# Float32 streaming-encoder trunk on one core: first products copied from PSUM to PSUM, one sum of weight quarters by an adding DMA, and the pools' first products moved

## The chip, the cores and the metric

The kernel runs on one core of a Trainium2 chip. The metric is device time of one execution in microseconds (us). Three executions of the kernel before took 709.14 to 709.78 us, median 709.22. TensorE (PE in the profile) multiplies 128x128 weight tiles with moving columns into PSUM, eight banks of 128x512 float32 each. VectorE (DVE), ScalarE (ACT) and GpSimd (POOL) work on elements; SyncE (SP) issues most DMAs.

## The reference

One layer over x of 512 tokens and 1024 channels, all in float32:

```
h = rmsnorm(x, norm_g)
a_u, a_v, a_z, b_p, b_z, c_h, c_b, c_c, c_z, gate_logits = split(h @ w_in)   # 9 x 1024 and 3 x 1024 columns
ya = spatial_gating(gelu(a_u), gelu(a_v), ...) * silu(a_z)
yb = multiscale_pool(b_p, pool_w, ...) * silu(b_z)      # trailing means over 2, 4, 8, 16 tokens, minus p, times pool_w
yc = c_b * causal_depthwise_conv(c_c * c_h, ...) * silu(c_z)
gates = sigmoid(gate_logits)                            # one of 1024 columns per branch
merged = gates_a * (ya @ w_branch_a) + gates_b * (yb @ w_branch_b) + gates_c * (yc @ w_branch_c)
out = rmsnorm(x + merged @ w_out, final_g)
```

## The kernel before, in words

Each float32 factor is split into a high part (hi, written by ScalarE as a cast, L59) and a low part (lo, the rest, written by VectorE, L60). A product is then three matmuls: hi by hi, hi by lo and lo by hi.

The wide product h @ w_in (except a_v) is made in 22 groups by `group` (L426 to L491). A group takes 2 x 128 output columns from each half of a 1024-column block, over all 1024 inputs, in a form with seven products instead of eight. Its weights are four quarters, a11, a12, a21 and a22, 128x1024 elements and 512 KB each, loaded by SyncE into the pool `wraw` (seven buffers, L62 to L65). The activations stand ready as seven combinations (b11, b21, t1 to t4, b22), each hi and lo. VectorE makes the combinations of weights: s1 = a21 + a22, a21' = a11 - a21, a11' = s1 - a11, a12' = a12 - a11' (L453 and L454). ScalarE and VectorE split each quarter or combination into `whi` and `wlo`, four buffers each. Each of the seven products is 24 matmuls of 256 columns (L437 to L443).

In order: b11 into bank px; ScalarE copies px to SBUF (c1, L447); b21 into its own bank py; VectorE adds c1 to py into the first quarter of the output (`plus`, L451); t2 is added on px, and ScalarE copies that (c2); t1 into pz; t3 added on px, copied (c3); VectorE adds c3 to pz; b22 added on pz, then c2 is added; t4 added on px, which ScalarE writes out. `use` (L483 to L490) is what a group does with its output: an activation by ScalarE, or, for cc, a product by VectorE.

`run` (L493) interleaves the groups: the b11 of a group comes before the late products b22 and t4 of the group ahead of it. Between some groups stand "other" steps: the mixing products of the branches. The order of groups is au0, az0, mix, au1, az1, mix, gates a0 with mixes, bp0, gates a1 with mixes (numbers 0 to 6, `mix` not counted), then bz0, bp1, pools' small products 0, bz1, pools' small products 1, gates b0 and b1 with mixes (7 to 11), then the eight groups of branch c (12 to 19) and its gates (20, 21). At the end come the product with w_out and the final norm. The instructions of each engine are put in order by the scheduler of the framework, which works from the dependences and its own estimates; only what goes through `pin` (the start) keeps the written order.

The pools (L654 to L675) are VectorE work on the output of bp; a pool's small product `pool_mm` (L685 to L710) is twelve matmuls, followed by two VectorE instructions and one of ScalarE for each tile. `keep_busy` (L157 to L161) is a run of matmuls of ones at the start.

Of the kernel before, what the change touches and what calls it, by code (L numbers as in the profile page):

```python
# [8 lines left out]
F32 = mybir.dt.float32  # L9
F32R = mybir.dt.float32r  # L10
AF = mybir.ActivationFunctionType
ALU = mybir.AluOpType
PSUM = bass.MemoryType.PSUM

P = 128
D = 1024
S = 512
KT = D // P
NB = S // P
HALF = 512  # L20
GC = 256
# [9 lines left out]
def mixers_kernel(ctx, tc, x, norm_g, w_in, sgu_ln_g, sgu_ln_b, sgu_w, sgu_b, pool_w, pool_b, pool_scale,  # L31
                  conv_w, conv_b, w_branch_a, w_branch_b, w_branch_c, w_out, final_g, out):
    nc = tc.nc
# [11 lines left out]
    wsum = ctx.enter_context(tc.tile_pool(name="wsum", bufs=2))  # L45
    whi = ctx.enter_context(tc.tile_pool(name="whi", bufs=4))
    wlo = ctx.enter_context(tc.tile_pool(name="wlo", bufs=4))
    outs = ctx.enter_context(tc.tile_pool(name="outs", bufs=3))
    part = ctx.enter_context(tc.tile_pool(name="part", bufs=3))
    tmp = ctx.enter_context(tc.tile_pool(name="tmp", bufs=4))  # L50
    small = ctx.enter_context(tc.tile_pool(name="small", bufs=4))
    psum = ctx.enter_context(tc.tile_pool(name="psum", bufs=8, space=PSUM))

    def bank():
        return psum.tile([P, 512], F32, tag="ps", name="ps")

    def split(hi, lo, src, keep=lambda ins: ins):

# [3 lines left out]
    def load_raw(src, shape):  # L62
        raw = wraw.tile([P, *shape], F32, tag="wraw", name="wraw")
        nc.sync.dma_start(out=raw, in_=src)
        return raw  # L65
# [68 lines left out]
    ones = const.tile([P, P], F32, name="ones")  # L134
# [14 lines left out]
    pin = tc.keep_in_program_order  # L149
# [7 lines left out]
    def keep_busy(n):  # L157
        for _ in range(n):
            pin(nc.tensor.matmul(idle[:, 0:P], lhsT=ones, rhs=ones, start=True, stop=True))  # L159

    keep_busy(6)  # L161
    gt_ps = bank()
    pin(nc.tensor.transpose(out=gt_ps[:, 0:KT], in_=g8, identity=ident[0:KT, 0:KT]))
    keep_busy(2)
# [173 lines left out]
    b11, b12, b22, b21 = (hsum[:, i] for i in range(4))  # L338
# [84 lines left out]
    def pair_of(ap):  # L423
        return ap.rearrange("p (j t) -> p j t", j=2)

    def group(c0, g, ct, use=None):  # L426
        def quarter(kh, nh):
            c = c0 + nh * HALF + g * GC
            return load_raw(w_in[kh * HALF : (kh + 1) * HALF, c : c + GC].rearrange("(k p) c -> p k c", p=P), [4, GC])

        def halved(raw):
            hi = whi.tile([P, 4, GC], F32R, tag="whi", name="whi")
            lo = wlo.tile([P, 4, GC], F32R, tag="wlo", name="wlo")
            split(hi, lo, raw)
            return hi, lo

        def product(a, b, ps, first):  # L437
            for j in range(2):
                for k in range(4):
                    for n, (x, y) in enumerate([(0, 0), (0, 1), (1, 0)]):  # L440
                        nc.tensor.matmul(ps[:, j * GC : (j + 1) * GC], lhsT=a[x][:, k, j * P : (j + 1) * P],  # L441
                                         rhs=moving[b][y][:, k, :], start=first and j == 0 and k == 0 and n == 0,
                                         stop=k == 3 and n == 2, skip_group_check=True)  # L443

        def copied(ps):
            s = part.tile([P, S], F32, tag="part", name="part")
            nc.scalar.copy(out=s, in_=ps)  # L447
            return pair_of(s)

        def plus(half, ts, s, ps):  # L450
            nc.vector.tensor_tensor(out=ct[:, half, :, ts], in0=pair_of(ps), in1=s, op=ALU.add)  # L451

        def sub(out, in0, in1, op=ALU.subtract):  # L453
            nc.vector.tensor_tensor(out=out, in0=in0, in1=in1, op=op)  # L454

        a11 = quarter(0, 0)
        f = halved(a11)
        px, py, pz = bank(), None, None
        product(f, "b11", px, True)
        yield  # L460
        c1 = copied(px)
        a12 = quarter(1, 0)
        f = halved(a12)
        a21, a22 = quarter(0, 1), quarter(1, 1)
        py = bank()
        product(f, "b21", py, True)
        plus(0, T1, c1, py)
        s1 = wsum.tile([P, 4, GC], F32, tag="wsum", name="s1")
        sub(s1, a21, a22, ALU.add)
        sub(a21, a11, a21)  # L470
        sub(a11, s1, a11)
        product(halved(a11), "t2", px, False)
        c2 = copied(px)
        pz = bank()
        product(halved(s1), "t1", pz, True)
        product(halved(a21), "t3", px, False)
        c3 = copied(px)
        sub(a12, a12, a11)
        plus(1, T2, c3, pz)
        yield  # L480
        product(halved(a12), "b22", pz, False)
        plus(0, T2, c2, pz)
        if use:  # L483
            use(ct[:, 0], 0, slice(0, S))
            use(ct[:, 1, :, T2], 1, T2)
        product(halved(a22), "t4", px, False)
        if use:
            use(pair_of(px), 1, T1)
        else:
            nc.scalar.copy(out=ct[:, 1, :, T1], in_=pair_of(px))  # L490
        yield  # L491

    def run(items):  # L493
# [153 lines left out]
    def pool_in(g):  # L647
        if not pads:
            make_pads()
        yield from group(OFF["bp"], g, Padded())  # L650
# [3 lines left out]
    def pools(g):  # L654
        if g == 0:
            early[0] = out_tile("d")
        for h in range(2):
            win = POOL_WINDOWS[g + 2 * h]
            for j in range(2):
                t = 4 * h + 2 * g + j  # L660
                pb = pads[h][:, j, :]
                cur, step = pb, 1
                while step < win:
                    nxt = tmp.tile([P, PAD + S], F32, tag="tmp", name="win")
                    lo = 2 * step - 1
                    nc.vector.tensor_add(out=nxt[:, lo:], in0=cur[:, lo:], in1=cur[:, lo - step : PAD + S - step])  # L666
                    cur, step = nxt, step * 2
                d = tile512("d") if g else early[0][:, h, j]
                nc.vector.scalar_tensor_tensor(out=d, in0=cur[:, PAD:], scalar=1.0 / win, in1=pb[:, PAD:],  # L669
                                               op0=ALU.mult, op1=ALU.subtract)  # L670
                dh = small.tile([P, PAD], F32, tag="dh", name="dh")
                nc.vector.tensor_mul(out=dh[:, :win], in0=cur[:, PAD : PAD + win], in1=rcount[:, :win])
                nc.vector.tensor_sub(out=d[:, :win], in0=dh[:, :win], in1=pb[:, PAD : PAD + win])
                if g:
                    split(y_hi[:, t, :], y_lo[:, t, :], d)  # L675
# [5 lines left out]
    def pool_z(g):  # L681
        silu_z[g] = out_tile("sz")
        yield from group(OFF["bz"], g, silu_z[g], act_into(silu_z[g], AF.Silu))
# [19 lines left out]
    def pool_mms(g):  # L703
        first = pool_mm(g)

        def after():
            first()
            pool_mm(g + 2)()

        return after  # L710

    for g in range(2):
# [5 lines left out]
    items.clear()  # L718
    y_hi, y_lo = y_tiles()
    early_split()  # L720
    items += [("group", pool_z(0), None), ("group", pool_in(1), lambda: pools(1)),
              ("other", lambda: pool_mms(0)), ("group", pool_z(1), None), ("other", lambda: pool_mms(1))]
    merge(1, w_branch_b[0])
    run(items)

# [114 lines left out]
```

## Time and profile before

| | |
|---|---|
| Median of three executions | 709.22 us (709.14 to 709.78) |
| Profiled execution, its own time | 708.7 us |
| Span from first to last instruction | 706.5 us |
| Mean granted TensorE clock | 0.992 |
| TensorE busy | 693.2 us, 4838 matmuls |
| VectorE busy | 537.6 us |
| ScalarE busy | 334.2 us |
| GpSimd busy | 15.0 us |

The profiled execution is one of several; its time is 0.5 us under the median. In a row of the timeline the first number is the start in us from the span's start, the second the duration, and the bracket at the end is how long the engine had waited and for what. Matmuls are pipelined, so that a row's duration is longer than the distance to the next start; time lost on TensorE is read from the distances between starts. An "x2" is two instructions in one row.

### The profile page before, as it was taken

How to read it: one execution, taken by the hardware profiler on the slowest of the kernel's cores; microseconds unless marked ns; L12 is line 12 of the kernel's file. 1: busy time of each engine (PE TensorE's matmuls, PEld its weight loads, DVE VectorE, ACT ScalarE, POOL GpSimd, SP SyncE). 2: the span in 40 equal slices, each digit the busy share in tenths (PEclk: the TensorE clock that was granted, in tenths of full speed). 3: DMA queues.
4: the chain of work that ended last, by engine and by line, in shares of the span. 5: the costliest groups of instructions: out<-in, count | busy, mean ns of one | idle time of the engine just before them, and what ended most of it. 6: DMA issues, size and time to landing. Idle time of an engine off the chain costs nothing.

```text
span 706.5 us, 11489 instructions
## 1 busy us (share of the span) xinstructions
PE 693.2 (98%) x4838; PEld 645.0 (91%) x4838; DVE 537.6 (76%) x618; ACT 334.2 (47%) x408; POOL 15.0 (2%) x38
## 2 busy tenths in 40 slices
PE   8999999999999999997999999999999999999996
PEld 6779999999899899997989899999999999898884
DVE  6998789795678685999665677798979985646453
ACT  6634556555244356455434334545545464234242
POOL 3001000000000000000000000000000000000001
PEclk9999999999999999998999999999999999999998
DMA  8721323315134113240515223234233334172002
GB/s 292 259 77 61 107 73 120 120 52 159 59 120 146 64 61 120 90 149 1 180 60 159 79 63 118 90 103 136 90 120 109 119 103 149 59 268 90 1 30 90
DMA packets 68536, 76.81 MB, mean 109 GB/s; under 512 B 2492, under 2 KB 61956, under 8 KB 68484
## 3 DMA queue, kind: packets, MB, share of 16 engines
q1 hardware_dynamic: 67892, 75.02, 32.8%
q10 hardware_dynamic: 592, 1.05, 0.4%
q8 instruction: 38, 0.62, 0.4%
q14 instruction: 14, 0.11, 0.0%
HBM read 73.96 MB, written 2.10 MB: 108 GB/s over the span
## 4 chain that ended last, share of the span: by engine, by line
PE 92%; DVE 5%; ACT 2%; issue 1%; POOLq 0%; DVEq 0%; ACTq 0%
PE ps L441 58%; PE ps L106 9%; PE ps L107 9%; PE ps L105 9%; PE ps L265 2%; DVE wlo L60 1%; PE ps L559 1%; DVE win L666 1%; PE ps L215 1%; PE ps L159 1%; DVE y L695 0%; DVE ylo L698 0%; ACT whi L232 0%; DVE d L669 0%; DVE ylo L60 0%
## 5 line engine op out<-in xcount | busy, mean ns | idle before, releaser
L59 ACT CAST whi<-wraw 128x1024 fp32r<-128x1024 f32 (+1 forms) x168 | 174.7, 1041 | 271.3 <-PE ps L441 170.7
L60 DVE TENSOR_TENSOR wlo<-wraw,whi 128x1024 fp32r<-128x1024 f32 (+1 forms) x168 | 201.5, 1207 | 79.4 <-ACT whi L59 79.2
L105 PE MATMUL ps<-yhi,whi 128*128 128x512 f32 x208 | 81.0, 389 | 0.0
L107 PE MATMUL ps<-yhi,wlo 128*128 128x512 f32 x208 | 81.0, 389 | 0.0
L106 PE MATMUL ps<-ylo,whi 128*128 128x512 f32 x208 | 81.0, 389 | 0.0
L441 PE MATMUL ps<-b21h,wlo 128*128 128x256 f32 x176 | 50.5, 287 | 3.9 <-DVE wlo L60 3.9
L454 DVE TENSOR_TENSOR wraw<-wraw 128x1024 f32<-128x1024 f32 x44 | 53.6, 1217 | 0.4
L441 PE MATMUL ps<-b22h,whi 128*128 128x256 f32 x176 | 50.7, 288 | 0.4 <-DVE sz L451 0.3
L441 PE MATMUL ps<-b21l,whi 128*128 128x256 f32 x176 | 50.5, 287 | 0.0
L441 PE MATMUL ps<-b21h,whi 128*128 128x256 f32 x176 | 50.2, 285 | 0.0
L441 PE MATMUL ps<-t2h,whi 128*128 128x256 f32 x176 | 49.6, 282 | 0.1
L441 PE MATMUL ps<-b11l,whi 128*128 128x256 f32 x176 | 49.6, 282 | 0.0
L441 PE MATMUL ps<-b22l,whi 128*128 128x256 f32 x176 | 49.6, 282 | 0.0
L441 PE MATMUL ps<-t2l,whi 128*128 128x256 f32 x176 | 49.6, 282 | 0.0
L441 PE MATMUL ps<-t1l,whi 128*128 128x256 f32 x176 | 49.6, 282 | 0.0
L441 PE MATMUL ps<-t3l,whi 128*128 128x256 f32 x176 | 49.6, 282 | 0.0
L441 PE MATMUL ps<-t4l,whi 128*128 128x256 f32 x176 | 49.6, 282 | 0.0
L441 PE MATMUL ps<-b11h,wlo 128*128 128x256 f32 x176 | 49.4, 281 | 0.2 <-DVE wlo L60 0.2
L441 PE MATMUL ps<-t2h,wlo 128*128 128x256 f32 x176 | 49.4, 281 | 0.0
L441 PE MATMUL ps<-t1h,whi 128*128 128x256 f32 x176 | 49.4, 281 | 0.0
L441 PE MATMUL ps<-t3h,whi 128*128 128x256 f32 x176 | 49.3, 280 | 0.0
L441 PE MATMUL ps<-t4h,whi 128*128 128x256 f32 x176 | 49.3, 280 | 0.0
(221 smaller groups left out, 1819.7 us busy)
## 6 DMA issues: line engine op xcount, KB each, us to landing
wraw<-in_w_in SPq DMA_DIRECT2D x96, 512.0 KB, 3.6
wraw<-in_w_branch_a SPq DMA_DIRECT2D x8, 512.0 KB, 3.4
wraw<-in_w_branch_b SPq DMA_DIRECT2D x8, 512.0 KB, 3.4
wraw<-in_w_branch_c SPq DMA_DIRECT2D x8, 512.0 KB, 3.5
wraw<-in_w_out SPq DMA_DIRECT2D x8, 512.0 KB
res<-in_x SPq DMA_DIRECT2D x4, 512.0 KB, 4.9
x_in<-in_x SPq DMA_DIRECT2D x3, 512.0 KB, 9.4
wraw<-in_pool_w SPq DMA_DIRECT2D x4, 256.0 KB, 2.7
```

What stands on the lines that cost most here:

```text
L59: keep(nc.scalar.copy(out=hi, in_=src))
L60: keep(nc.vector.tensor_tensor(out=lo, in0=src, in1=hi.bitcast(F32), op=ALU.subtract))
L105: nc.tensor.matmul(ps, lhsT=a[0], rhs=b[0], start=first, stop=False)
L106: nc.tensor.matmul(ps, lhsT=a[0], rhs=b[1], start=False, stop=False)
L107: nc.tensor.matmul(ps, lhsT=a[1], rhs=b[0], start=False, stop=last)
L159: pin(nc.tensor.matmul(idle[:, 0:P], lhsT=ones, rhs=ones, start=True, stop=True))
L215: pin(nc.tensor.transpose(out=ps[:, k * P : (k + 1) * P], in_=hns[b][:, kk * P : (kk + 1) * P], identity=ident))
L265: pin(nc.tensor.matmul(vps[b], lhsT=a, rhs=r, start=done[b] == 1, stop=done[b] == 3 * KT))
L441: nc.tensor.matmul(ps[:, j * GC : (j + 1) * GC], lhsT=a[x][:, k, j * P : (j + 1) * P], rhs=moving[b][y][:, k, :], start=first and j == 0 a ...
L454: nc.vector.tensor_tensor(out=out, in0=in0, in1=in1, op=op)
L559: nc.tensor.matmul(mx[:, n * P : (n + 1) * P], lhsT=v_t[:, n, t * P : (t + 1) * P], rhs=wsT[:, t, :], start=True, stop=True)
L666: nc.vector.tensor_add(out=nxt[:, lo:], in0=cur[:, lo:], in1=cur[:, lo - step : PAD + S - step])
```

## The change

Three things change in `group`. ScalarE copies the first product, px, into a bank of a pool of its own (py, two banks `psum_add`; the pool `psum` has six instead of eight), and the product b21 is made with `start=False` on top of it, so that c1 and the addition on VectorE go away, and `use` or ScalarE's copy reads the bank directly (`out_or_use`). `use` of the first half is therefore two calls of 512 columns, not one of 1024. And s1 is no longer added by VectorE: SyncE loads the quarter a21 a second time, into s1, and GpSimd issues a DMA of a22 that adds onto it. The pool `part` has two buffers instead of three.

At the start the six matmuls of ones become eight, which write the two add banks whole. In the list of the pool branch the pools' first small products stand ahead of group bp1 instead of behind it. The scratch of DMA descriptors has 2048 instead of 1024 bytes.

```diff
--- before.py
+++ after.py
@@ -46,13 +46,18 @@
     whi = ctx.enter_context(tc.tile_pool(name="whi", bufs=4))
     wlo = ctx.enter_context(tc.tile_pool(name="wlo", bufs=4))
     outs = ctx.enter_context(tc.tile_pool(name="outs", bufs=3))
-    part = ctx.enter_context(tc.tile_pool(name="part", bufs=3))
+    part = ctx.enter_context(tc.tile_pool(name="part", bufs=2))
     tmp = ctx.enter_context(tc.tile_pool(name="tmp", bufs=4))
     small = ctx.enter_context(tc.tile_pool(name="small", bufs=4))
-    psum = ctx.enter_context(tc.tile_pool(name="psum", bufs=8, space=PSUM))
+    psum = ctx.enter_context(tc.tile_pool(name="psum", bufs=6, space=PSUM))
+
+    psum_add = ctx.enter_context(tc.tile_pool(name="psum_add", bufs=2, space=PSUM))
 
     def bank():
         return psum.tile([P, 512], F32, tag="ps", name="ps")
+
+    def add_bank():
+        return psum_add.tile([P, 512], F32, tag="pa", name="pa")
 
     def split(hi, lo, src, keep=lambda ins: ins):
 
@@ -158,7 +163,10 @@
         for _ in range(n):
             pin(nc.tensor.matmul(idle[:, 0:P], lhsT=ones, rhs=ones, start=True, stop=True))
 
-    keep_busy(6)
+    for _ in range(2):
+        pa = add_bank()
+        for n in range(4):
+            pin(nc.tensor.matmul(pa[:, n * P : (n + 1) * P], lhsT=ones, rhs=ones, start=n == 0, stop=n == 3))
     gt_ps = bank()
     pin(nc.tensor.transpose(out=gt_ps[:, 0:KT], in_=g8, identity=ident[0:KT, 0:KT]))
     keep_busy(2)
@@ -424,9 +432,12 @@
         return ap.rearrange("p (j t) -> p j t", j=2)
 
     def group(c0, g, ct, use=None):
+        def source(kh, nh):
+            c = c0 + nh * HALF + g * GC
+            return w_in[kh * HALF : (kh + 1) * HALF, c : c + GC].rearrange("(k p) c -> p k c", p=P)
+
         def quarter(kh, nh):
-            c = c0 + nh * HALF + g * GC
-            return load_raw(w_in[kh * HALF : (kh + 1) * HALF, c : c + GC].rearrange("(k p) c -> p k c", p=P), [4, GC])
+            return load_raw(source(kh, nh), [4, GC])
 
         def halved(raw):
             hi = whi.tile([P, 4, GC], F32R, tag="whi", name="whi")
@@ -447,6 +458,12 @@
             nc.scalar.copy(out=s, in_=ps)
             return pair_of(s)
 
+        def out_or_use(ps, half, ts):
+            if use:
+                use(pair_of(ps), half, ts)
+            else:
+                nc.scalar.copy(out=ct[:, half, :, ts], in_=pair_of(ps))
+
         def plus(half, ts, s, ps):
             nc.vector.tensor_tensor(out=ct[:, half, :, ts], in0=pair_of(ps), in1=s, op=ALU.add)
 
@@ -455,18 +472,19 @@
 
         a11 = quarter(0, 0)
         f = halved(a11)
-        px, py, pz = bank(), None, None
+        px = bank()
         product(f, "b11", px, True)
         yield
-        c1 = copied(px)
+        py = add_bank()
+        nc.scalar.copy(out=py, in_=px)
         a12 = quarter(1, 0)
         f = halved(a12)
+        s1 = wsum.tile([P, 4, GC], F32, tag="wsum", name="s1")
+        nc.sync.dma_start(out=s1, in_=source(0, 1))
+        nc.gpsimd.dma_start(out=s1, in_=source(1, 1), accum_op=ALU.add)
         a21, a22 = quarter(0, 1), quarter(1, 1)
-        py = bank()
-        product(f, "b21", py, True)
-        plus(0, T1, c1, py)
-        s1 = wsum.tile([P, 4, GC], F32, tag="wsum", name="s1")
-        sub(s1, a21, a22, ALU.add)
+        product(f, "b21", py, False)
+        out_or_use(py, 0, T1)
         sub(a21, a11, a21)
         sub(a11, s1, a11)
         product(halved(a11), "t2", px, False)
@@ -481,13 +499,10 @@
         product(halved(a12), "b22", pz, False)
         plus(0, T2, c2, pz)
         if use:
-            use(ct[:, 0], 0, slice(0, S))
+            use(ct[:, 0, :, T2], 0, T2)
             use(ct[:, 1, :, T2], 1, T2)
         product(halved(a22), "t4", px, False)
-        if use:
-            use(pair_of(px), 1, T1)
-        else:
-            nc.scalar.copy(out=ct[:, 1, :, T1], in_=pair_of(px))
+        out_or_use(px, 1, T1)
         yield
 
     def run(items):
@@ -718,8 +733,8 @@
     items.clear()
     y_hi, y_lo = y_tiles()
     early_split()
-    items += [("group", pool_z(0), None), ("group", pool_in(1), lambda: pools(1)),
-              ("other", lambda: pool_mms(0)), ("group", pool_z(1), None), ("other", lambda: pool_mms(1))]
+    items += [("group", pool_z(0), None), ("other", lambda: pool_mms(0)), ("group", pool_in(1), lambda: pools(1)),
+              ("group", pool_z(1), None), ("other", lambda: pool_mms(1))]
     merge(1, w_branch_b[0])
     run(items)
 
@@ -823,7 +838,7 @@
     import concourse.bacc as bacc
     from concourse.bass_utils import run_bass_kernel_spmd
 
-    nc = bacc.Bacc("TRN2", target_bir_lowering=False, num_devices=1, dynamic_dma_scratch_size=1024)
+    nc = bacc.Bacc("TRN2", target_bir_lowering=False, num_devices=1, dynamic_dma_scratch_size=2048)
     arrays, args = {}, {}
     for name in _INS:
         a = np.ascontiguousarray(inputs[name])
```

The first place is ScalarE around group 2 (au1, the first group behind a mixing step). `ps` and `pa` are banks, `part` the copies in SBUF, `s1` the sum, `sz` the output of the group ahead of it, `yhi` its high part. ScalarE's rows before:

```order
L520 ACTIVATE sz_800<-ps_807 128x2x256
L59 CAST whi_1227<-s1_1192 128x1024
L59 CAST whi_1255<-wraw_1162 128x1024
L59 CAST yhi_632<-sz_800 128x1024 x2
L447 COPY part_1154<-ps_1129 128x512
```

And in the changed kernel:

```order
L64 CAST whi_1234<-s1_1169 128x1024
L535 ACTIVATE sz_807<-ps_814 128x2x256
L64 CAST yhi_639<-sz_807 128x1024
L64 CAST whi_1262<-wraw_1172 128x1024
L64 CAST yhi_639<-sz_807 128x1024
L479 COPY pa_1161<-ps_1136 128x512
```

The copy of the first product stays behind the same weight cast and behind the casts of `yhi`, one of which has moved ahead of the weight cast.

The second place is TensorE at the same group. Here `ps_1129` and `ps_1136` are px, `ps_1166` is py before and `pa_1161` after, `ps_1233` is pz. The end of b11 before:

```order
L441 MATMUL ps_1129<-b11h_163,whi_1125 128x256
L441 MATMUL ps_1129<-b11l_164,whi_1125 128x256
L441 MATMUL ps_1129<-b11h_163,wlo_1126 128x256
L441 MATMUL ps_1166<-b21h_165,whi_1158 128x256
L441 MATMUL ps_1166<-b21l_166,whi_1158 128x256
L441 MATMUL ps_1166<-b21h_165,wlo_1159 128x256
```

And in the changed kernel:

```order
L452 MATMUL ps_1136<-b11h_170,whi_1132 128x256
L452 MATMUL ps_1136<-b11l_171,whi_1132 128x256
L452 MATMUL ps_1136<-b11h_170,wlo_1133 128x256
L452 MATMUL ps_1233<-t1h_430,whi_1234 128x256
L452 MATMUL ps_1233<-t1l_431,whi_1234 128x256
L452 MATMUL pa_1161<-b21h_172,whi_1165 128x256
L452 MATMUL pa_1161<-b21l_173,whi_1165 128x256
L452 MATMUL pa_1161<-b21h_172,wlo_1166 128x256
```

Two matmuls of t1 have come between b11 and b21; b21 now writes the bank that the copy writes.

The third place is ScalarE at group 10 (gates b0), right behind the pools' last small products; `y` is such a product with gate and bias. Before:

```order
L520 ACTIVATE sz_3137<-sz_3137 128x1024
L697 ACTIVATE yhi_2576<-y_3382,pvec_442 128x512
L697 ACTIVATE yhi_2576<-y_3386,pvec_442 128x512
L447 COPY part_3450<-ps_3425 128x512
L697 ACTIVATE yhi_2576<-y_3410,pvec_442 128x512
L697 ACTIVATE yhi_2576<-y_3414,pvec_442 128x512
L59 CAST whi_3492<-wraw_3419 128x1024
```

And in the changed kernel:

```order
L535 ACTIVATE sz_3034<-ps_3041 128x2x256
L712 ACTIVATE yhi_2583<-y_3389,pvec_449 128x512
L712 ACTIVATE yhi_2583<-y_3393,pvec_449 128x512
L712 ACTIVATE yhi_2583<-y_3417,pvec_449 128x512
L479 COPY pa_3457<-ps_3432 128x512
L712 ACTIVATE yhi_2583<-y_3421,pvec_449 128x512
L64 CAST whi_3499<-wraw_3426 128x1024
```

The copy now stands behind three of the four writes of `yhi` instead of two, and four products' writes are left around group 10 as before, the other four having moved to the time around group 8.

## Rows read from the trace of the kernel before

**Rows 1.** Page: busy us, share of the span and instructions of each engine.

```profile
PE 693.2 (98%) x4838; PEld 645.0 (91%) x4838; DVE 537.6 (76%) x618; ACT 334.2 (47%) x408; POOL 15.0 (2%) x38
```

**Rows 2.** Table by stretches: length, busy us by engine, then clock, DMA share, GB/s.

```profile
core 0: us, PE busy (x) PEld busy (x) DVE busy (x) ACT busy (x) POOL busy (x), PEclk, DMA share, GB/s
...
110.00:160.00 50.00, 49.92 (x423) 49.51 (x422) 44.32 (x46) 29.80 (x35) 0.25 (x2) 1.00 0.31 99
...
315.00:335.00 20.00, 15.97 (x102) 15.00 (x102) 19.70 (x28) 11.66 (x16) 0.00 (x0) 0.83 0.09 27
```

**Rows 3.** Timeline of TensorE at group 2: start, duration, engine, line, operation.

```profile
104.67 0.28 PE L441 MATMUL ps<-b11l,whi 128*128 128x256 f32 x1
...
106.55 0.28 PE L441 MATMUL ps<-b11h,wlo 128*128 128x256 f32 x1
...
109.97 0.28 PE L441 MATMUL ps<-t1l,whi 128*128 128x256 f32 x1
110.29 0.39 PE L441 MATMUL ps<-t2h,whi 128*128 128x256 f32 x1
110.51 0.28 PE L441 MATMUL ps<-t2l,whi 128*128 128x256 f32 x1
```

**Rows 4.** Timeline of TensorE in the pool branch.

```profile
312.96 0.28 PE L441 MATMUL ps<-t4h,wlo 128*128 128x256 f32 x1
313.54 0.39 PE L441 MATMUL ps<-b22h,whi 128*128 128x256 f32 x1 [0.30 <-DVE sz L451]
...
322.03 0.28 PE L441 MATMUL ps<-b21l,whi 128*128 128x256 f32 x1
322.46 0.39 PE L441 MATMUL ps<-b11h,wlo 128*128 128x256 f32 x1 [0.15 <-DVE wlo L60]
...
325.04 0.28 PE L441 MATMUL ps<-b11h,wlo 128*128 128x256 f32 x1
329.20 0.58 PE L441 MATMUL ps<-b21h,wlo 128*128 128x256 f32 x1 [3.88 <-DVE wlo L60]
...
334.06 0.32 PE L441 MATMUL ps<-t2h,whi 128*128 128x256 f32 x1
```

**Rows 5.** Timeline of VectorE in the pool branch.

```profile
327.93 1.21 DVE L60 TENSOR_TENSOR wlo<-wraw,whi 128x1024 fp32r<-128x1024 f32 x1
```

**Rows 6.** Table by stretches, around the stop in the pool branch.

```profile
325.00:327.20 2.20, 0.32 (x3) 0.11 (x1) 1.97 (x4) 1.36 (x3) 0.00 (x0) 1.00 0.00 0
327.40:334.00 6.60, 4.80 (x22) 4.80 (x23) 6.53 (x7) 2.49 (x3) 0.00 (x0) 0.50 0.00 0
```

**Rows 7.** Groups of instructions: busy us, mean ns, idle before and its releaser.

```profile
L454 DVE TENSOR_TENSOR s<-wraw 128x1024 f32<-128x1024 f32 x22 | 26.9, 1221 | 12.7 <-DMA wraw<-in_w_in 12.7
```

**Rows 8.** Timeline of VectorE at group 2.

```profile
111.12 0.69 DVE L451 TENSOR_TENSOR gu<-ps,part 128x512 f32<-128x512 f32 x1
```

**Rows 9.** Timeline of TensorE at group 11.

```profile
372.89 0.28 PE L441 MATMUL ps<-b11h,wlo 128*128 128x256 f32 x1
```

**Rows 10.** Timeline of ScalarE at group 11.

```profile
373.14 1.05 ACT L59 CAST whi<-wraw 128x1024 fp32r<-128x1024 f32 x1 [1.88 <-PE ps L441]
374.10 0.58 ACT L447 COPY part<-ps 128x512 f32<-128x512 f32 x1
```

**Rows 11.** Timeline of ScalarE at group 2.

```profile
106.81 1.05 ACT L59 CAST whi<-wraw 128x1024 fp32r<-128x1024 f32 x1 [1.12 <-PE ps L441]
107.76 2.00 ACT L59 CAST yhi<-sz 128x1024 fp32r<-128x1024 f32 x2
109.67 0.57 ACT L447 COPY part<-ps 128x512 f32<-128x512 f32 x1
```

**Rows 12.** Timeline of TensorE at the start.

```profile
1.05 2.93 PE L159 MATMUL ps<-ones 128*128 128x128 f32 x12 [1.05 <-DVE warm L139]
```

**Rows 13.** Page: DMA queues and issues; packets, MB, share; size, us to landing.

```profile
q1 hardware_dynamic: 67892, 75.02, 32.8%
...
wraw<-in_w_in SPq DMA_DIRECT2D x96, 512.0 KB, 3.6
```

## The prediction

> **What bounds the kernel now.** I read the busy table first [rows 1]: TensorE is busy for 693.2 of 706.5 us, VectorE for 76%. Little can be won by making VectorE's work smaller as such; what counts is where TensorE stands still. The table by stretches shows where that is [rows 2]: in a typical stretch, 110 to 160 us, it is busy for 49.92 of 50 us, and only 315 to 335 us stands out: 15.97 of 20 us, VectorE at 19.70 and the granted clock at 0.83. That is the pool branch. Matmuls of 256 columns start 0.1175 us apart when nothing holds them (16 steps from 104.67 to 106.55 [rows 3]). By that pitch the rows of TensorE in the pool branch [rows 4] tell how much is lost there: 0.46 us is lost between 312.96 and 313.54, 0.31 between 322.03 and 322.46, and 4.04 between 325.04 and 329.20. VectorE was working through the pools' results and wrote the low part that TensorE waited for only at 327.93 to 329.14 [rows 5]. After it, 23 matmuls take from 329.20 to 334.06, 4.86 us instead of 2.70, because the granted clock is 0.50, 1.2 instead of 2.4 GHz [rows 6]: 2.16 lost. The first matmul after a stop holds the next one up by about 0.1 (110.29 to 110.51 [rows 3]); with three of these the stretch loses 7.3 us, and nearly everything else is matmul time that the change keeps.
>
> **What the change takes away.** From VectorE: 22 sums of two quarters (26.9 us in all [rows 7]) and 22 additions of a copied first product to the second (0.69 us each, as the one at 111.12 [rows 8]), together 42 of its 537.6 us. None of that is a gain by itself, since TensorE is full. It pays only where VectorE is late, which is the pool stretch. There also the pools' first small products move ahead of pool group 1, so that the two batches of VectorE work no longer come together. Between them these should free the stretch: +7.3 us at most.
>
> **What it adds on TensorE's path.** The first product of a group is now copied by ScalarE from one PSUM bank into another, and the second product (b21) is added on top of that copy. In the old form b21 went to a bank of its own and needed nothing. Now b21's first matmul waits until b11 is done and the copy is done. Where a previous group's late products (48 matmuls, 5.64 us by the pitch) stand between b11 and b21, the copy is hidden. By the written order this is so in twelve of the 22 groups. In the other ten (groups 0, 2, 4, 5, 7, 8, 10, 11, 12, 21, those behind a mixing step or at the start of a list) nothing of another group stands there, and the program puts only some matmuls of t1 between as a cover: 13 of them in six groups, 14 in group 4, 2 in groups 2 and 8, none in group 10. On ScalarE the copy is not first either: the cast that takes the weight buffer which b11 frees stands ahead of it, as the order of group 2 shows.
>
> Six seams with 13 matmuls (0, 5, 7, 11, 12, 21). I take group 11 of before as the model. Its last b11 matmul starts at 372.89 [rows 9], so b11 ends at 373.01 by the pitch. The cast starts at 373.14, the copy at 374.10, and the copy ends at 374.68 [rows 10]. TensorE can start about 0.05 after that (at group 2: copy's end 110.24, next matmul 110.29 [rows 3, 11]), so 1.72 us after b11's end. Thirteen matmuls cover 13 x 0.1175 = 1.53. About 0.15 each, between 0 and 0.3 with the slow first matmul: 0.8 in all (0 to 1.8).
>
> Group 2. There ScalarE also has a cast of the branch result between that cast and the copy. In the trace: b11 ends at 106.67, the cast starts at 106.81, two casts of the branch result at 107.76, the copy at 109.67 for 0.57 [rows 3, 11]. In the new order one of the two stands ahead of the weight cast, one behind. So 0.14 + 0.95 + 0.96 + 0.57 + 0.05 = 2.67, less 2 x 0.1175: TensorE stands still for 2.43 us, 2.5 with the slow first matmul; I take 2.7, since the first of those two casts needs a VectorE product made just before it. What is behind the waiting b21 on TensorE is the rest of the group, so all of it counts.
>
> Group 4. The same chain in the new order, and the same three instructions in the trace before; less 14 x 0.1175 = 1.65 the 2.67 leave 1.02, 1.2 with the restart and the same doubt.
>
> Group 8. Cast and copy as in group 11, 1.72, less 0.235: 1.5 at least. Besides, its VectorE work waits for quarters whose load is issued late, because their buffers come free late; up to 1 us more. I take 2.2 (1.4 to 2.7).
>
> Group 10, and what stays of the pool stretch. No cover at all: b21 waits for a copy of 0.58 that stands behind a ScalarE write of the pools' result, and the low part of t2's weights comes from VectorE right after. With one such write (about the 0.6 to 0.7 of a copy of that shape), one copy and half a low part (1.21 [rows 5]) this is an estimate of 2.0 to 2.1 us. The ends are 0, if VectorE gets ahead, and 5, if most of the present 4.04 with its lower clock stays.
>
> Start. Eight matmuls of the warm-up instead of six: 12 records for six take 2.93 us [rows 12], so two more cost 0.98. The chain to the first real work, from the mean square over rstd to hn, has its own path over VectorE and GpSimd and hides a part: 0.8 (0.2 to 1.0).
>
> In the old form groups 2 and 4 lost some already, as t2 waited for the copy of b11's bank (110.29 against 109.97, 0.2 with the pitch taken off; 0.3 with the restart [rows 3]), and group 4 as much: those waits go into the new ones: 0.6 gained.
>
> **The new DMA sum.** A quarter is loaded by SyncE straight into the sum's buffer and GpSimd issues a second load that is added to it: 22 x 2 x 512 KB, 23 MB beside the 75 that the load queue moves in 32.8% of the engines' time [rows 13]. GpSimd is busy for 15 us in all [rows 1], so nothing of weight is queued behind its wait for the first load. The plain load of a quarter takes 3.6 us to land [rows 13]; the adding one is not in this trace. The sum's two buffers are asked for about one group ahead (168 matmuls, 19.7 us by the pitch), so it may take three times as long and cost nothing. I take nothing; the other end is the third rival.
>
> **The sum.** Costs 0.8 + 2.7 + 1.2 + 2.2 + 2.1 + 0.8 = 9.8; gains 7.3 + 0.6 = 7.9. Net +1.9 us, on the profiled execution of 708.7 us 710.6; the runs shown have their median 0.5 higher, 709.22, so 711.1, rounded to 711.0. A ScalarE copy from PSUM into PSUM is in no row here; the copy into SBUF is, at 0.58 [rows 10], and I take that.
>
> The Trainium skill ("ScalarE: Activation LUTs", "Step-by-step: what each stage is for") says that ScalarE writes faster into PSUM than into SBUF. No row here shows it. By that rule the six seams would come out nearer 0 than 0.8, and the time nearer 710.
>
> **Rivals.** First, faster: VectorE, freed of 42 us, is over 1 us ahead at the seams, so that the casts before the copy never wait for its results. Group 8 falls to 1.3, group 4 to 1.0, group 2 to 2.4, group 10 to 0.7, with 0.8 and 0.8 as before: 7.0. The gain rises to about 8.9, as waits of b22 for VectorE's additions go too ([rows 4] shows one of 0.46). Net -1.9: 707.3. It decides where the pool stretch is free of VectorE altogether. For it speaks that VectorE is at 19.70 of 20 us there [rows 2] and is rid of a sum of 1.2 and an addition of 0.7 in each group; against it that the ScalarE chain at groups 2 and 4 doesn't depend on VectorE.
>
> Second, slower: the clock falls at the new stops. In the trace it had fallen about 2.0 us after TensorE fell idle at 325.3 (last matmul 325.04 for 0.28 [rows 4]; the clock is 1.00 to 327.2 and 0.50 from 327.4 on [rows 6]), and the stop of group 2 is 2.4 us long, that of group 8 about 2. Each fall would cost about the 2.16 of [rows 4]: 713.3 for one, 715.5 for two. It decides from a stop of about 2 us on. Against it: one stop doesn't tell whether a stop of 2.4 is enough each time.
>
> The rule behind it in the Trainium skill ("TensorE: Matmul & The Clock Gate", "Part 1: The HAM clock gate") is that the array's clock is halved after idling and comes back only after sustained work. The trace agrees: 0.50 between 327.4 and 334.0, through 4.9 us of work after the restart at 329.2 [rows 4, 6].
>
> Third: the adding loads are slow or delay the plain ones. VectorE already waited 12.7 us for quarters in its 22 sums [rows 7]. If the new loads bring that much again and half of it reaches TensorE, 6.4 more: 717.
>
> Fourth: the pool stretch does not get free because VectorE's pool work itself is as long as before, and of the 7.3 only 4 are gained, as half of the stop (2.0) stays with part of its slow clock (1.3): 711.1 + 3.3 = 714.4.
>
> **How the numbers follow.** What a measurement of this kernel can tell from no change is about 0.2%, 1.4 us: below 707.8 is faster, above 710.6 slower. The forecast (709.8 to 712.3) has 0.42, the faster rival 0.27, the clock 0.18, slow loads 0.06, the unfreed stretch 0.07. Of the forecast's 0.42 some 0.22 lie under 710.6; a part of the faster rival (0.02) ends within 0.2% as well. So faster 0.25, same 0.25, slower 0.50. The range from 706.0 to 715.5 leaves out slow loads and the ends of the faster rival and of two clock falls; the forecast's own is 709.5 to 712.5.
>
> **What would show it.** In the profile after: TensorE waiting for ScalarE's copy at b21 of groups 2 and 4 for about 2.4 and 1.0 us; the stretch of the pools with less than 3 us lost and its clock at 1.00; VectorE busy for about 496 us; a granted clock below 1.00 around group 2 if the second rival holds. I am wrong if b21 never waits for the copy, or if the pool stretch still has a stop of 4 us, or if a new wait for a load appears on VectorE.

## The result, and the profile after

The changed kernel is slower: five executions took 713.51 to 718.63 us, median 716.11, against 709.22 before; the ratio is 1.0087 (95% interval 1.0069 to 1.0105), 6.2 us on 709.22. The direction was the one forecast; the size, 711.0, was too small by 4 us (715.4 by the ratio) to 5 us (by the median). The executions also lie wider apart than the five of before in the same session (5 us instead of 0.9; in two later sessions 27 executions each of the kernel before lay within 3.1 and 2.3 us). The first profile is of the fastest of them, span 711.7 us against 706.5.

The page of that profile answers to [rows 1] and [rows 13]: first busy time by engine, then the DMA queues (packets, MB, share of 16 engines) and the issues (count, size, median us from issue to landing).

```profile
PE 694.4 (98%) x4842; PEld 642.8 (90%) x4842; DVE 500.9 (70%) x578; ACT 337.1 (47%) x426; POOL 43.8 (6%) x60
...
q1 hardware_dynamic: 79508, 86.55, 38.1%
q0 software_dynamic: 11616, 11.54, 10.6%
...
wraw<-in_w_in SPq DMA_DIRECT2D x96, 512.0 KB, 4.1
s<-in_w_in SPq DMA_DIRECT2D x22, 512.0 KB, 3.7
s<-in_w_in POOLq DMA_DIRECT2D x22, 512.0 KB, 6.5
```

VectorE lost 37 us and TensorE is as full as before. The adding loads took 6.5 us to land against 3.7 of the plain ones into the same buffer, and 10.6% of the DMA engines' time for 11.5 MB, where the plain queue moves 86.6 MB in 38.1%.

The table by stretches, with the columns of [rows 2], shows three places of the same kernel: group 2, group 8 and the end of the pool branch.

```profile
103.00:111.20 8.20, 5.47 (x47) 5.26 (x45) 8.20 (x10) 6.20 (x8) 0.00 (x0) 1.00 0.00 0
...
281.00:289.00 8.00, 5.78 (x41) 5.11 (x40) 8.00 (x11) 6.12 (x8) 0.00 (x0) 1.00 0.00 0
320.00:340.00 20.00, 18.94 (x135) 17.17 (x134) 19.48 (x30) 12.88 (x19) 0.00 (x0) 1.00 0.25 81
```

The pool stretch has become what was hoped for, 18.94 of 20 us busy at full clock where [rows 2] had 15.97 at 0.83. But two places that lost nothing of note before now stand still for 2.7 and 2.2 us. TensorE's timeline names what they wait for (groups 2, 8, 10 and 11, in the order of time):

```profile
108.19 0.28 PE L452 MATMUL ps<-t1l,whi 128*128 128x256 f32 x1
111.22 0.38 PE L452 MATMUL pa<-b21h,whi 128*128 128x256 f32 x1 [2.76 <-ACT pa L479]
...
285.63 0.28 PE L452 MATMUL ps<-t1l,whi 128*128 128x256 f32 x1
288.13 0.39 PE L452 MATMUL pa<-b21h,whi 128*128 128x256 f32 x1 [2.22 <-ACT pa L479]
...
333.73 0.28 PE L452 MATMUL ps<-b11h,wlo 128*128 128x256 f32 x1
334.67 0.39 PE L452 MATMUL pa<-b21h,whi 128*128 128x256 f32 x1 [0.66 <-ACT pa L479]
...
378.15 0.28 PE L452 MATMUL ps<-t1h,whi 128*128 128x256 f32 x1
378.46 0.38 PE L452 MATMUL pa<-b21h,whi 128*128 128x256 f32 x1
378.69 0.28 PE L452 MATMUL pa<-b21l,whi 128*128 128x256 f32 x1
```

By the pitch of 0.1175 us these are 2.92, 2.39, 0.82 and 0.19 us lost (worked out with unrounded starts; the two decimals of the rows can shift a value by 0.01), and 0.11 more each for the slow first matmul (378.46 to 378.69). ScalarE at group 2 shows the chain of [rows 11] in its new order:

```profile
107.37 1.05 ACT L64 CAST yhi<-sz 128x1024 fp32r<-128x1024 f32 x1 [0.20 <-DVE sz L565]
108.33 1.04 ACT L64 CAST whi<-wraw 128x1024 fp32r<-128x1024 f32 x1
109.64 1.04 ACT L64 CAST yhi<-sz 128x1024 fp32r<-128x1024 f32 x1 [0.28 <-DVE sz L565]
110.59 0.58 ACT L479 COPY pa<-ps 128x512 f32<-128x512 f32 x1
```

Cast, cast, copy, and TensorE starts 0.05 us after the copy's end. The two short waits for VectorE (0.20 and 0.28) are what lifts the stop from the 2.43 that the chain alone would give to 2.92.

At group 8 something else stands in front. b11 ends at 285.26 there, and ScalarE writes two of the pools' results before it comes to the cast and the copy:

```profile
285.28 1.38 ACT L712 ACTIVATE yhi<-y,pvec 128x512 fp32r<-128x512 f32 x2
286.57 1.03 ACT L64 CAST whi<-wraw 128x1024 fp32r<-128x1024 f32 x1
287.50 0.58 ACT L479 COPY pa<-ps 128x512 f32<-128x512 f32 x1
```

These are the writes that came to this place with the pools' first small products.

### The profile page after: what moved, and what is told of

Same layout as the page of the kernel before. It is cut to its first block, busy times and chain, and to the rows that moved or that the text cites. A ratio compares the mean times of both kernels' runs of the same rounds, so it can differ in the third digit from the quotient of the medians.

```text
span 711.7 us, 11609 instructions
## 1 busy us (share of the span) xinstructions
PE 694.4 (98%) x4842; PEld 642.8 (90%) x4842; DVE 500.9 (70%) x578; ACT 337.1 (47%) x426; POOL 43.8 (6%) x60
## 3 DMA queue, kind: packets, MB, share of 16 engines
q1 hardware_dynamic: 79508, 86.55, 38.1%
q0 software_dynamic: 11616, 11.54, 10.6%
## 4 chain that ended last, share of the span: by engine, by line
PE 54%; DVE 4%; issue 1%; ACT 0%; POOLq 0%
PE ps L452 30%; PE ps L112 6%; PE ps L111 6%; PE ps L110 6%; PE pa L452 5%; DVE wlo L65 1%; DVE win L681 1%; DVE y L710 0%; DVE ylo L713 0%; DVE d L684 0%; DVE wraw L471 0%; DVE ylo L65 0%; POOLq L848 0%; ACT o L826 0%; DVE ppad L468 0%
## 5 line engine op out<-in xcount | busy, mean ns | idle before, releaser
L484 POOL DMA_DIRECT2D s<-in_w_in x22 | 28.8, 1308 | 486.4 <-DMA s<-in_w_in 252.4
L452 PE MATMUL pa<-b21h,whi 128*128 128x256 f32 x176 | 50.2, 285 | 5.8 <-ACT pa L479 5.6
L452 PE MATMUL ps<-t1h,wlo 128*128 128x256 f32 x176 | 49.4, 281 | 0.9 <-DVE wlo L65 0.9
L452 PE MATMUL pa<-b21l,whi 128*128 128x256 f32 x176 | 49.6, 282 | 0.0
L452 PE MATMUL pa<-b21h,wlo 128*128 128x256 f32 x176 | 49.3, 280 | 0.0
```

The source lines that it names most:

```text
L484: nc.gpsimd.dma_start(out=s1, in_=source(1, 1), accum_op=ALU.add)
```

## The experiments

Ratios are to the kernel before on the same chip, with 95% intervals. **Theory 1** is that of the prediction: TensorE waits at b21 for ScalarE's copy at the ten seams, and the pool stretch gets free. **Theory 2**, the rival: the adding DMAs' traffic makes it slow. A third theory, that both do, is added with the kernel with own banks below.

**One part at a time.** First the move alone:

```diff
-    items += [("group", pool_z(0), None), ("group", pool_in(1), lambda: pools(1)),
-              ("other", lambda: pool_mms(0)), ("group", pool_z(1), None), ("other", lambda: pool_mms(1))]
+    items += [("group", pool_z(0), None), ("other", lambda: pool_mms(0)), ("group", pool_in(1), lambda: pools(1)),
+              ("group", pool_z(1), None), ("other", lambda: pool_mms(1))]
```

> The kernel before with only the pools' first small products moved ahead of group bp1. Theory 1 (TensorE waits at b21 for ScalarE's copy at the seams; the pool stretch is a VectorE problem that the move and the relief of VectorE cure): 703 to 707 us, the stop of 4.0 us at about 325 us and its lower clock gone or under 1.5 us. Theory 2 (the adding DMAs' traffic makes the change slow): says nothing of the traffic here, and if the move alone does not help, 708 to 710.

Measured: 708.53 us (707.41 to 709.75), ratio 0.9984 (0.9975 to 0.9992). A miss of theory 1: the move alone wins 1 us, not 3 to 6. TensorE's old stop is gone, but a new one of 3.22 us stands a little later, at t2 of group 10 (first fence), with the granted clock at 0.50 for 3.4 us behind it; VectorE's timeline shows the chain in front of it (second fence):

```profile
328.38 0.28 PE L441 MATMUL ps<-b21h,wlo 128*128 128x256 f32 x1
331.72 0.38 PE L441 MATMUL ps<-t2h,whi 128*128 128x256 f32 x1 [3.06 <-ACT whi L59]
```

```profile
325.60 1.22 DVE L454 TENSOR_TENSOR s<-wraw 128x1024 f32<-128x1024 f32 x1
326.73 0.75 DVE L698 SCALAR_TENSOR_TENSOR ylo<-y,pvec,yhi 128x512 fp32r<-128x512 f32 x1
327.39 1.22 DVE L454 TENSOR_TENSOR wraw<-wraw 128x1024 f32<-128x1024 f32 x1
328.77 0.69 DVE L451 TENSOR_TENSOR gate<-ps,part 128x512 f32<-128x512 f32 x1 [0.15 <-PE ps L441]
329.37 1.21 DVE L454 TENSOR_TENSOR wraw<-s,wraw 128x1024 f32<-128x1024 f32 x1
```

Here the sum (1.22) and the addition (0.69) that the other two parts take away do stand in the way. This is where the parts of the change help each other.

The DMA sum alone:

```diff
-        s1 = wsum.tile([P, 4, GC], F32, tag="wsum", name="s1")
-        sub(s1, a21, a22, ALU.add)
+        s1 = wsum.tile([P, 4, GC], F32, tag="wsum", name="s1")
+        nc.sync.dma_start(out=s1, in_=source(0, 1))
+        nc.gpsimd.dma_start(out=s1, in_=source(1, 1), accum_op=ALU.add)
```

> The kernel before with only the sum s1 made by the plain load and the adding DMA (descriptor scratch 1216 bytes so that three part buffers still fit). Theory 1: 704 to 709 us, since VectorE loses 27 us of work and the DMA sum is a group ahead. Theory 2: 712 us or more, with a spread between executions as in the changed kernel (713.5 to 718.6), and TensorE waiting for low parts that wait for loads.

Measured: 711.81 us (708.40 to 714.23), ratio 1.0029 (1.0012 to 1.0046). Between the theories: the median is where neither put it, the spread is theory 2's. The profile, of an execution of 708.75 us, has the pool stop unchanged, at 326.48 to 330.64 and with the same releaser, although VectorE is busy for 24 us less (513.2 instead of 537.6):

```profile
326.48 0.28 PE L444 MATMUL ps<-b11h,wlo 128*128 128x256 f32 x1
330.64 0.58 PE L444 MATMUL ps<-b21h,wlo 128*128 128x256 f32 x1 [3.88 <-DVE wlo L60]
```

The PSUM addition alone (the parts of the diff on `add_bank`, `out_or_use`, `use` and the start):

> The kernel before with only the copy from PSUM to PSUM and b21 added on top (six and two banks, eight warm-up matmuls, use in halves); the sum stays on VectorE and the pools' order as before. Theory 1: 713 to 718 us: seams with 13 or 14 matmuls of cover 0.3 and 1.1 us each, a wait at b21 for the copy, and the pool stretch mostly as before. Theory 2: 707 to 711 us, as the traffic is that of before.

Measured: 718.12 us (717.67 to 719.15), ratio 1.0119 (1.0106 to 1.0132). This is 0.1 us over theory 1's range and far from theory 2's. The part costs most: 0.2 us at each of six seams, 1.07 each at groups 2 and 4 (there for the low part of s1, which VectorE writes late, not for the copy), and a stop of 3.40 us at t2 of group 10 behind which the granted clock is 0.50 for 6.8 us.

Move and DMA sum together, without the PSUM addition:

> The kernel before with the move and the DMA sum, without the PSUM addition. Theory 1: 701 to 704.5 us, nothing waits for the copy and the pool stretch is free. Theory 2: 709 us or more, the gain of the pool stretch eaten by loads that come late.

Measured: 708.92 us (707.59 to 712.93), ratio 0.9995 (0.9982 to 1.0009). A miss of theory 1, and within 0.1 us of theory 2's range. In the profile, of an execution of 708.60 us, the stop in the pool stretch is 2.6 us in three pieces instead of 4.0, but the clock is still at 0.50 for 3.4 us behind it, and VectorE waits 23.0 us for quarters against 12.7 in the kernel before. Most of the hoped-for gain is missing.

The changed kernel without the move:

> The changed kernel with the pools' first small products back behind group bp1. If the pool stretch is cured by the move (with VectorE's relief): 718 to 722 us, the stop of about 4 us back at the pools. If VectorE's relief alone cures it: 713 to 717, as the changed kernel.

Measured: 722.75 us (721.19 to 724.22), ratio 1.0179 (1.0156 to 1.0203). The stop of 4.03 us at the pools is back, so the move is needed to cure it. With the other two parts it is worth 0.8 to 0.9 per cent (1.0179 against 1.0101 in the same session and 1.0087 in the first), alone 0.2.

**The seams taken away.** In the ten groups in which nothing of another group stands between b11 and b21 the old form is kept (`own` is true there); everything else is the changed kernel:

```diff
-        py = add_bank()
-        nc.scalar.copy(out=py, in_=px)
+        if own:
+            c1 = copied(px)
+        else:
+            py = add_bank()
+            nc.scalar.copy(out=py, in_=px)
...
-        product(f, "b21", py, False)
-        out_or_use(py, 0, T1)
+        if own:
+            py = bank()
+            product(f, "b21", py, True)
+            plus(0, T1, c1, py)
+        else:
+            product(f, "b21", py, False)
+            out_or_use(py, 0, T1)
```

> The changed kernel, but in the ten groups where nothing of another group stands between b11 and b21 the old form is kept: copy to SBUF, b21 in a bank of its own, addition on VectorE. Theory 1 (what the change costs is TensorE waiting at those ten seams for ScalarE's copy): 705 to 710 us, some 8 us under the changed kernel's 716.1, no wait of over 0.4 us at any b21. Theory 2 (the adding DMAs' traffic costs it): 712 us or more. Theory 3 (both: the seams some 8 us, the DMA sum some 2 and the spread): 707 to 710 with executions 3 us or more apart.

Measured: 708.67 us (707.23 to 710.91), ratio 0.9987 (0.9977 to 0.9997). The seams are worth 1.0 per cent, 7 us: theory 1 in its main point. Theory 3 fits as well, its spread too (3.7 us between executions). The six banks, the two `part` buffers, the start and the descriptor scratch are those of the changed kernel here, so none of them can be what makes the change 6 us slower. At group 2 the wait is now t2's, and small:

```profile
110.79 0.28 PE L452 MATMUL ps<-b21h,wlo 128*128 128x256 f32 x1
111.24 0.39 PE L452 MATMUL ps<-t2h,whi 128*128 128x256 f32 x1 [0.17 <-ACT part L458]
```

The same with the sum back on VectorE (descriptor scratch 1024 as before):

> As the kernel with own banks at the ten seams, and the sum s1 back on VectorE. Theory 1: like that kernel or up to 2 us slower, since VectorE has 27 us more to do in the pool stretch. Theory 3: 1 to 3 us faster than that kernel in the median, and executions within 2 us of each other.

Measured: 709.25 us (708.45 to 710.91), ratio 0.9996 (0.9987 to 1.0004). Once the seams are gone the DMA sum costs nothing that can be told: the two intervals overlap, and theory 3's second half (1 to 3 us faster without it) does not hold here. So what that DMA costs is not the same in every kernel; that it hangs on what stands behind the late quarter is an argument, not shown.

**More cover instead.** All of t1 is written ahead of b21:

```diff
+        pz = bank()
+        product(halved(s1), "t1", pz, True)
         product(f, "b21", py, False)
         out_or_use(py, 0, T1)
...
-        pz = bank()
-        product(halved(s1), "t1", pz, True)
```

> The changed kernel with all 24 matmuls of t1 written ahead of b21 in every group: 24 x 0.1175 = 2.82 us of cover against a chain of 1.7 to 2.7 us from b11's end to the copy's end. Theory 1: all seams but group 10 free, 705 to 711 us. Theory 2: as the changed kernel, 714 to 718.

Measured: 722.61 us (722.01 to 725.08), ratio 1.0189 (1.0173 to 1.0204). A clear miss. b21 hardly waits any more, but now the copies of the later sums have no cover. The groups of weight loads on TensorE show it (busy us, mean ns, idle before and its releaser):

```profile
L452 PEld LDWEIGHTS ps<-t4h,whi 128*128 128x128 f32 x176 | 33.4, 190 | 5.1 <-ACT part L458 5.1
...
L452 PEld LDWEIGHTS pa<-b21h,whi 128*128 128x128 f32 x176 | 33.1, 188 | 0.6 <-ACT pa L479 0.6
L452 PEld LDWEIGHTS ps<-t3h,whi 128*128 128x128 f32 x176 | 33.1, 188 | 7.0 <-ACT part L458 6.8
```

The t1 matmuls had covered the copy of px between t2 and t3. They can be spent once: in the changed kernel the weight loads were idle for 7.7 us ahead of b21, 1.7 ahead of t3 and nothing ahead of t4; here it is 0.6, 7.0 and 5.1. The rest of the 6.5 us between the two medians was not followed up; this profile also has a wait of b22 of group 4 for VectorE, 2.42 us, with the clock at 0.50 for 3.4 us behind it.

**The adding itself.** The kernel with only the DMA sum, but the second load plain:

```diff
-        nc.gpsimd.dma_start(out=s1, in_=source(1, 1), accum_op=ALU.add)
+        nc.gpsimd.dma_start(out=s1, in_=source(1, 1))
```

> The kernel with only the DMA sum, but GpSimd's second load into s1 is plain and doesn't add (so s1 is a22 and not a21 + a22, and the result is not the reference's). If the adding (reading the target back) is what costs and spreads: 707 to 709.5 us, within 2 us of each other. If the second queue or the 23 MB more of loads is: 710 to 713 and executions 4 us or more apart, as with the adding.

Measured: 708.41 us (708.15 to 711.62, nine of eleven under 709), ratio 0.9988 (0.9978 to 0.9997): 2.9 us less than with the adding, for the same bytes on the same queue. The same edit in the changed kernel:

> The changed kernel with GpSimd's second load plain, not adding (s1 is a22 alone, so the result is not the reference's). If the adding makes the spread and some 2 to 3 us, as the pair of DMA-only kernels says: 712 to 714.5 us and executions within 2 us. If the seams' stops and the clock make it: 714 to 718 with the same spread.

Measured: 712.92 us (712.77 to 714.59), ratio 1.0047 (1.0029 to 1.0064), against 1.0087 and, in the same session, 1.0101 with the adding: 3 to 4 us. It is the adding, not the number of bytes or the queue. The DMA view of the same 15 us, 86 to 101, in the changed kernel and then in this one (share of the 16 engines in this window; size; us to landing):

```profile
q0 software_dynamic: 528, 0.52, 22.9%
...
s<-in_w_in POOLq DMA_DIRECT2D x1, 512.0 KB, 7.5
```

```profile
q0 software_dynamic: 144, 0.52, 11.2%
...
s<-in_w_in POOLq DMA_DIRECT2D x1, 512.0 KB, 4.1
```

For the same half megabyte the adding load goes out in 528 packets instead of 144, which take twice the engine time, and it takes 3.4 us longer to land. Over the whole execution VectorE waits 11.8 us for quarters with the adding and 8.7 without (the pair without the move and the PSUM addition: 20.1 and 12.2).

The seam of group 2 shows it too. With the plain load ScalarE's casts of `yhi` no longer wait for VectorE, and b21 loses 2.37 us instead of 2.92, about what the chain alone would give:

```profile
108.25 0.28 PE L452 MATMUL ps<-t1l,whi 128*128 128x256 f32 x1
110.74 0.39 PE L452 MATMUL pa<-b21h,whi 128*128 128x256 f32 x1 [2.21 <-ACT pa L479]
```

**A longer execution seen.** The changed kernel once more:

> The changed kernel once more, for a second profile: its first profile was of the fastest of five executions (713.5 of 713.5 to 718.6), with no fall of the clock inside. Expected: 714 to 718 us, the same waits at the seams (2.9 us at group 2, 2.4 at group 8), and in a slower execution one or two stretches of 3.4 or 6.8 us at a granted clock of 0.50 behind one of these stops, 1.5 to 3 us more, or VectorE waiting longer for loads. If neither is seen, the spread has another cause.

Measured: 717.30 us (715.57 to 718.39), ratio 1.0101 (1.0076 to 1.0125), and the profile is of an execution of 717.13 us, span 715.3. Two differences to the first profile, one behind the other, make 2.7 of the 3.6 us. VectorE waits longer for a quarter; here the same instruction in the first profile, in the second, and with the plain load, one fence each:

```profile
97.61 1.23 DVE L471 TENSOR_TENSOR wraw<-wraw 128x1024 f32<-128x1024 f32 x1 [1.31 <-DMA wraw<-in_w_in]
```

```profile
99.72 1.23 DVE L471 TENSOR_TENSOR wraw<-wraw 128x1024 f32<-128x1024 f32 x1 [2.83 <-DMA wraw<-in_w_in]
```

```profile
96.81 1.22 DVE L471 TENSOR_TENSOR wraw<-wraw 128x1024 f32<-128x1024 f32 x1
```

The addition that b22 of group 1 needs stands behind it, so b22 loses 1.96 us in the longer execution and 0.44 in the first. Then the stop at group 2 is 2.92 us in both, but in the longer one the clock falls behind it (TensorE first, then the table by stretches):

```profile
101.61 0.39 PE L452 MATMUL ps<-b22h,whi 128*128 128x256 f32 x1 [1.81 <-DVE sz L468]
...
110.31 0.28 PE L452 MATMUL ps<-t1l,whi 128*128 128x256 f32 x1
113.34 0.39 PE L452 MATMUL pa<-b21h,whi 128*128 128x256 f32 x1 [2.76 <-ACT pa L479]
```

```profile
113.70:117.10 3.40, 3.40 (x19) 3.40 (x18) 3.40 (x4) 0.00 (x0) 0.00 (x0) 0.50 0.48 152
```

In 3.4 us 19 matmuls start instead of 29: some 1.2 us lost. So the clock rival is real, but not in every execution. The kernel without the move has the same pair in its profile, 1.94 us lost at b22 and 2.92 at group 2, and its clock stays at 1.00 there; what decides is not shown.

**An attempt to use only what helps.** The move, and the adding DMA in groups 9 and 10 alone:

> The kernel with the move alone, and the DMA sum only in groups 9 and 10 (bz1 and gates b0), where VectorE's sum of 1.22 us stands in the chain that t2 of group 10 waited for (a stop of 3.22 us in the kernel with the move alone). If the adding DMA costs only where a quarter's load is late behind it, and the sum matters only here: the stop falls to about 2 us and the clock's fall behind it may go, 705.5 to 708 us, executions within 2 us. If any adding DMA costs: 708.5 or more.

Measured: 713.32 us (711.93 to 713.78), ratio 1.0036 (1.0022 to 1.0050). The hoped-for branch is missed. The stop at t2 of group 10 did fall, to 2.6 us in three pieces. But the first of the two adding loads goes out at 267 us, and VectorE waits for a plain quarter for 6.17 us, twice the longest such wait in the kernel before, 3.0 (first fence, VectorE); t2 of group 8 then loses 2.55 us (second, TensorE), and the clock is at 0.50 behind it (third, table by stretches):

```profile
276.17 1.23 DVE L457 TENSOR_TENSOR wraw<-wraw 128x1024 f32<-128x1024 f32 x1 [6.17 <-DMA wraw<-in_w_in]
```

```profile
284.54 0.28 PE L444 MATMUL ps<-b21h,wlo 128*128 128x256 f32 x1
287.20 0.58 PE L444 MATMUL ps<-t2h,whi 128*128 128x256 f32 x1 [2.39 <-ACT whi L59]
```

```profile
287.00:293.80 6.80, 6.39 (x26) 5.81 (x27) 5.95 (x6) 2.99 (x4) 0.00 (x0) 0.50 0.46 133
```

So one adding load can cost more than it gains where the next quarter is wanted soon after, at least by this one profile. No kernel of these is clearly better than the one before: the best that compute the reference, the move alone and the own banks at the seams, are 0.1 to 0.2 per cent faster.

## Why the prediction was right and where it fell short

Right, in its own steps: b21 waits for the copy at the seams; group 2 lost 3.0 us (2.7 predicted), group 4 1.2 (1.2), group 8 2.8 with the slow starts ahead of it (2.2), group 10 and the rest of the pool stretch 1.9 (2.1). At group 4 the wait is for the low part of s1 by VectorE, not for the copy (at 155.75, 0.89 us), so there the size was right by luck. At group 8 the reason given, quarters that come late, was not what was seen: the two writes of the pools' results stood in front, 1.3 us. The 7.3 us of the pool stretch went, as said; the experiments show that the move is needed for it, and that the other two parts shorten the chain that is left. VectorE came down to 500.9 (about 496 said).

Too small, in the first profile by 3.1 us. The six seams with 13 matmuls lost 0.30 each, 1.8 in all, the upper end of the range given: I had 0.15. Groups 2 and 8 gave 0.9 more than forecast; the start and group 10 were the other way, 0.3 instead of 0.8 and 0.2 less. A cost of those covers was missing: the 13 t1 matmuls drawn ahead of b21 were missing between t2 and t3, where they had covered the copy c2, and t3 now waits for that copy in those six groups. Its weight loads were idle for 1.7 us in all, against 0.0 before; by the distances between starts TensorE lost 1.4, slow starts included:

```profile
L452 PEld LDWEIGHTS ps<-t3h,whi 128*128 128x128 f32 x176 | 33.1, 188 | 1.7 <-ACT part L458 1.7
```

With the 0.55 of b22 at 99.5 (0.44 and a slow start) the costs come to 13.0; less the 7.9 gained that is +5 us for the first profile, which shows 711.7 - 706.5 = 5.2.

The step that failed is "I take nothing" for the new DMA sum. The argument was that the sum's buffer is asked for a group ahead. That was true and beside the point: s1 itself was not late, the plain quarter behind it was. The sign that the prediction had set itself, a new wait for a load on VectorE, is in both profiles (at 97.61 and 99.72). The third rival named this with a chance of 0.06 and 6.4 us; the pairs with and without the adding put it at 3 to 4 us in the changed kernel, part of it through the waits for loads shown above and, as it may be, part through a fall of the clock behind the stop at group 2. The one fall seen cost 1.2 us, where the clock rival had 2.16.

How the two divide over all executions stays open, since only two of them have a profile. Each execution's mean granted clock, which is on record, tells a little: it was 0.997 in the profile without a fall and 0.995 in the one with a fall. Of the nine executions of the changed kernel two have 0.997 (713.51 and 715.57 us), the other seven 0.992 to 0.995 (715.66 to 718.63); of the four with the plain load three have 0.997 (712.77 to 712.95) and one 0.994 (714.59). So the adding costs about 0.6 to 2.7 us where no fall shows, and the falls come on top; that they are more frequent with it is likely, but these are few executions.

The prediction's range ended at 715.5, its time for two clock falls, and left slow loads out. That 715.4, the time by the ratio, lies inside it, and the median of 716.11 only just outside, is therefore luck in part.

The ScalarE rule that the prediction drew on, from the Trainium skill ("ScalarE: Activation LUTs", "Step-by-step: what each stage is for"), did not show here: the 22 copies from PSUM to PSUM took 579 ns in the mean, and the 44 copies of the same shape to SBUF 580; the measured times decide, and the rule changed nothing here:

```profile
L458 ACT COPY part<-ps 128x512 f32<-128x512 f32 x44 | 25.5, 580 | 0.0
...
L479 ACT COPY pa<-ps 128x512 f32<-128x512 f32 x22 | 12.7, 579 | 0.9 <-PE ps L452 0.9
```

## What to carry to other kernels

Work taken off an engine that is not the bound is worth what stands in the chain of a wait, and a sum added onto a copy turns a free product into one that waits: look at what the copying engine has queued ahead of it, and at what stands on TensorE meanwhile. Cover is spent once; matmuls drawn ahead of one wait are missing at the next. A DMA that adds is to be priced by what it does to the loads beside it, not by when its own result is wanted.

## What had not been expected of the hardware

The adding load of 512 KB took twice the engine time of the plain one (22.9 against 11.2% of 15 us) in 528 instead of 144 packets. And the same stop of 2.92 us was followed by a fall of the granted clock to 0.50, 1.2 GHz, in one profile and not in the two others that have it, so a stop of that length costs either itself or about 1.2 us more.
